# Moving tile addresses in a two-layer decoder trunk: large tiles on multiples of 2048 bytes, fourteen operand tiles in steps of 4128

## The chip, the cores and the metric

The kernel runs on one core of one Trainium2 chip. The metric is device microseconds of one execution; a run's figure is the median of several executions, and one separate execution is profiled.

## The reference

A decoder trunk on x of 512 tokens by 1024 channels, float32, two layers. Each layer is a half-step SwiGLU FFN, a token mixer, and a second half-step FFN:

```python
for layer in range(2):
    x = x + 0.5 * swiglu(rmsnorm(x, ffn_norm[layer, 0]), ffn_w_in[layer, 0], ffn_w_out[layer, 0])
    h = rmsnorm(x, mix_norm[layer])
    y = hybrid_mixer(h, ...) if layer == 0 else stick_breaking(h, ...)
    x = x + y
    x = x + 0.5 * swiglu(rmsnorm(x, ffn_norm[layer, 1]), ffn_w_in[layer, 1], ffn_w_out[layer, 1])
```

`swiglu(h)` is `(silu(a) * b) @ w_out` with `a, b` the halves of `h @ w_in`, 2816 wide. The hybrid mixer runs an RG-LRU recurrence beside forgetting attention with 8 heads; the other mixer is stick-breaking attention with 16 heads. Both attentions are causal.

## The kernel before

Everything is kept transposed: channels on the 128 partitions, the 512 tokens along the free dimension. x lies in eight tiles `x0` to `x7`. Every float32 operand is split into a high and a low part (`hi`/`lo` of weights, `h`/`l` or `xh`/`xl` of activations), and one product is three matmuls: high by high, high by low, low by high. The stationary operand of each is a 128x128 block of a weight tile, newly loaded for each matmul, and the moving operand is an activation tile; in the token products (`g_tok`, L241 to L243) it is the other way round.

The program is a row of stages: ffn(0), hybrid, ffn(1), ffn(2), stick, ffn(3). Inside each, TensorE's order is written out by hand (`manual_schedule`); the other engines follow by data.

- **ffn.** The hidden dimension is 22 blocks `j` of 128. Blocks 0 to 3 (`plain`) are ordinary products by `mm3` (L125 to L127) with moving operands of 512 columns. Blocks 4 to 21 come in nine pairs, each by seven products (`product`, L450) after Strassen's scheme: the operands `ops[0]` to `ops[6]` are computed once per ffn (`put`, `less`, `quarter`) and kept in fourteen tiles `t0h`, `t0l` to `t6h`, `t6l` of 128 x (4 x 256) floats; the weight sums are formed on VectorE per pair. One `product` is 24 matmuls of 256 columns. Between products come output units (`outputs`) for an earlier chunk: twelve matmuls of 512 columns by `mm3` per unit (eighteen in the last chunk), with hidden tiles `g` (and `sum` for blocks 20 and 21) as the moving operand.
- **hybrid and stick.** Projections as fill (`g_proj` L222 to L224 with 512 moving columns, `g_tok` L241 to L243 with 256 or 264), between the steps of `attend` (scores, transposes L639, `weigh` L657).
- `rstd_parts` (L163) multiplies sums of squares by a column of ones: a matmul of one column, with a full 128x128 weight load before each.

**Where tiles lie.** A tile's byte address within each partition follows from the order of the pools and, in a pool, from the order in which tags are first used; each slot is rounded up to 32 bytes. The first pool, `const`, begins at 1152 and ends at 3360. Then come `state` (x, `xh`, `xl`, `sq`, `acc`, two small `rt`, `rb`), `wp` (`raw`, `hi`, `lo`, 4096 bytes a slot), and the pool of the stage. So, modulo 2048:

| tiles | address mod 2048 | mod 512 |
|---|---|---|
| x, xh, xl, sq, acc; g of blocks 4 to 15 (they take the slots of xh, xl) | 1312 | 288 |
| weights raw, hi, lo; in the ffn: ab, a21, a22, sum, p5, the t tiles, g of blocks 0 to 3 and 16 to 19 | 1376 | 352 |
| hybrid and stick: many residues, as small and odd-sized tiles lie between large ones (tt of stick 1696, of hybrid 1792; v 1440) | | |

Blocks of a weight tile and quarters of a t tile start a multiple of 512 bytes into their tile, so the residue modulo 512 is the same for all blocks of one tile.

Of the kernel before, what the change touches and what calls it, by code (L numbers as in the profile page):

```python
# [10 lines left out]
F32 = mybir.dt.float32  # L11
F32R = mybir.dt.float32r
# [4 lines left out]
P = 128  # L17
S = 512
# [4 lines left out]
NB = S // P  # L23
HD = 64
# [12 lines left out]
QK0 = 80  # L37
FB0 = 82
NPAR = 90
NQF = 256 + H_FOX  # L40


# [25 lines left out]
def kernel(ctx: ExitStack, tc: tile.TileContext, x, par, ffn_in, ffn_in2, ffn_out, ffn_out2,  # L68
                      hy_ug, hy_qkv, hy_qf, rg_w, hy_out, sb_qk, sb_v, sb_out, out):
    nc = tc.nc  # L70
    V, A, G, T, SY = nc.vector, nc.scalar, nc.gpsimd, nc.tensor, nc.sync

    const = ctx.enter_context(tc.tile_pool(name="const", bufs=1))
    state = ctx.enter_context(tc.tile_pool(name="state", bufs=1))
    wp = ctx.enter_context(tc.tile_pool(name="wp", bufs=1))
    ps = ctx.enter_context(tc.tile_pool(name="ps", bufs=1, space=PSUM))
# [81 lines left out]
    def rstd_parts():  # L158

        pt = psum("t", 2)  # L160
        for tb in range(NB):
            for i, sq in enumerate(acc):
                T.matmul(out=pt[:, tb:tb + 1], lhsT=sq[:, tb * P:(tb + 1) * P], rhs=ones, start=i == 0, stop=i == 1)  # L163
        rt = state.tile([P, NB], F32, tag="rt", bufs=2, name="rt")
        V.tensor_scalar(out=rt, in0=pt[:, :NB], scalar1=1.0 / D, scalar2=EPS, op0=ALU.mult, op1=ALU.add)
        G.tensor_tensor(out=rt, in0=rt, in1=mhalf[:, :NB], op=ALU.pow)

        def rest():
            pb = psum("t", 2)
            for tb in range(NB):  # L170
                T.transpose(out=pb[:, tb * P:(tb + 1) * P], in_=rt[:, tb:tb + 1].broadcast_to([P, P]),
                            identity=ident)
            rb = state.tile([P, S], F32, tag="rb", bufs=1, name="rb")
            A.copy(out=rb, in_=pb)
            return rt, rb

        return rest
# [147 lines left out]
    def ffn(f, g_next, last=False):  # L325
# [2 lines left out]

        with ExitStack() as es:
            gp = es.enter_context(tc.tile_pool(name=f"ffn{f}", bufs=1))  # L330
            hid = {}
            ops = {}

            def slot(o, c, dt):

                return gp.tile([P, 4, 256], dt, tag=f"t{o}{c}", bufs=1, name=f"t{o}{c}")

            def temp(tag, dt=F32):
                return gp.tile([P, 2, S], dt, tag=tag, bufs={"sum": 4, "ab": 2}[tag], name=tag)
# [352 lines left out]
    def hybrid(g_next):  # L692
        with ExitStack() as es:
            mp = es.enter_context(tc.tile_pool(name="hy", bufs=1))

            def wk(tag, dt=F32, bufs=1):
                return mp.tile([P, S], dt, tag=tag, bufs=bufs, name=tag)

            rt = rb = None
# [4 lines left out]
            def r_in(i):  # L704
                def evac_u(pt):
                    nonlocal rt, rb
                    if rt is None:
                        rt, rb = rstd()
                    u = mp.tile([P, S + 4], F32, tag="u", bufs=2, name="u")
                    G.memset(u[:, 0:3], 0.0)  # L710
                    V.tensor_tensor(out=u[:, 3:3 + S], in0=pt, in1=rb, op=ALU.mult)
                    st[i] = [u]

                def evac_g(pt):
                    gs = wk("gs", bufs=2)
                    V.tensor_tensor(out=gs, in0=pt, in1=rb, op=ALU.mult)
                    st[i].append(gs)

                return [(1, 24 * US_512, g_proj(hy_ug[i + 4 * j], e, on_x, KT)) for j, e in enumerate((evac_u, evac_g))]

            def r_chain(i):

                u, gs = st[i]
                wraw = mp.tile([P, 2, P], F32, tag="wgr", name="wgr")
                wh = mp.tile([P, 2, P], F32R, tag="wgh", name="wgh")
                wl = mp.tile([P, 2, P], F32R, tag="wgl", name="wgl")
                G.memset(wraw, 0.0)
                for hb in range(2):
                    sl = slice(hb * HD, (hb + 1) * HD)
# [20 lines left out]
                o = wk("o")  # L750
# [6 lines left out]
                t = wk("c1")  # L757
                b = wk("c2")
# [53 lines left out]
            def forget():  # L812
                n = H_FOX
                ft, sp, sm, ww, pp = (f_in[0][:, 32 * q:32 * q + 32] for q in range(5))
                A.activation(out=sp, in_=ft, func=AF.Abs)
                A.activation(out=sm, in_=sp, func=AF.Sigmoid, scale=-1.0)
                A.activation(out=sp, in_=sp, func=AF.Sigmoid)
                log1p_exp(sp, sm, ww, pp)
                V.tensor_scalar(out=ft, in0=ft, scalar1=-1.0, scalar2=0.0, op0=ALU.mult, op1=ALU.max)
                yield  # L820
                V.tensor_tensor(out=ft, in0=ft, in1=sm, op=ALU.add)
                row = mp.tile([P, 6], F32, name="row")
                for r in range(4):
                    V.tensor_reduce(out=row[:, r:r + 1], in_=ident[:, r::32], axis=AX.X, op=ALU.add)
                for c in range(2):
                    V.tensor_tensor(out=row[:, 4 + c:5 + c], in0=row[:, 2 * c:2 * c + 1],
                                    in1=row[:, 2 * c + 1:2 * c + 2], op=ALU.add)
                V.tensor_scalar(out=row[:, 5:6], in0=row[:, 5:6], scalar1=-1.0, scalar2=None, op0=ALU.mult)
                for t in range(2):
                    nl = wk("ge" if t else "xc").rearrange("p (b g r) -> p b g r", b=NB, g=4)  # L830
                    V.tensor_copy(out=nl, in_=ft.rearrange("p (b h) -> p b h", h=n)[:, :, 4 * t:4 * t + 4]
                                  .unsqueeze(3).broadcast_to([P, NB, 4, 32]))
                    for _ in range(1 if t else HY_FORGET):
                        yield
                    pn = psum("t", 2)
                    for tb in range(NB):
                        T.transpose(out=pn[:, tb * P:(tb + 1) * P], in_=nl[:, tb].rearrange("p g r -> p (g r)"),
                                    identity=ident)
                    yield
                    nf, hi, mix = wk("c1"), wk("c2", F32R), wk("o")  # L840
                    V.tensor_tensor_scan(out=nf, data0=ones.broadcast_to([P, S]), data1=pn, initial=0.0,
                                         op0=ALU.mult, op1=ALU.add)
                    A.copy(out=hi, in_=nf)
                    V.tensor_tensor(out=nf, in0=nf, in1=hi.bitcast(F32), op=ALU.subtract)
                    for dst, r, c in ((fb[t], 0, 5), (fa[t], 2, 4)):
                        A.activation(out=mix, in_=hi.bitcast(F32), func=AF.Identity, scale=row[:, r:r + 1],
                                     bias=row[:, c:c + 1])
                        V.scalar_tensor_tensor(out=dst, in0=nf, scalar=row[:, r + 1:r + 2], in1=mix,
                                               op0=ALU.mult, op1=ALU.add)
                        yield  # L850
# [19 lines left out]
            def qk_unit(half, which, dst):  # L870
                qs = []

                def evac(tb, pt):
                    nonlocal rt, rb
                    if rt is None:
                        rt, rb = rstd()
# [1 line left out]
                        forget_in(tb, pt[:, 256:])  # L878
                        pt = pt[:, :256]
                    q = mp.tile([P, 256], F32, tag="q", bufs=8, name="q")  # L880
                    sq = mp.tile([P, 256], F32, tag="e0", bufs=1, name="sqq")
                    ss = mp.tile([P, 4], F32, tag="ss", bufs=4, name="ss")
                    rc = rt[:, tb:tb + 1]
                    A.activation(out=sq, in_=pt, func=AF.Square, scale=rc)
                    V.tensor_reduce(out=ss, in_=heads(sq), axis=AX.X, op=ALU.add)
# [41 lines left out]
            ls = {}  # L927

            def score(p, hb, b):
                n = (b + 1) * P  # L930
                if (hb, b) == (0, 0):
                    ls[p] = mp.tile([P, 2, NB], F32, tag="ls", bufs=2, name="ls")
                sp = pso()
                bs = slice(b * P, n)
                q2, k2 = (second[w][p % 2][hb] for w in range(2))
# [1 line left out]
                T.matmul(out=sp[:, bs], lhsT=identr, rhs=mask_c, start=False, stop=False, skip_group_check=True)  # L937
                T.matmul(out=sp[:, :n], lhsT=q2[:, bs], rhs=k2[:, :n], start=False, stop=True)
                sc = mp.tile([P, S], F32, tag="sc", bufs=3, name="sc")[:, :n]
                m = mp.tile([P, 1], F32, tag="m", bufs=4, name="m")  # L940
                V.tensor_reduce(out=m, in_=sp[:, :n], axis=AX.X, op=ALU.max, negate=True)
                A.activation(out=sc, in_=sp[:, :n], func=AF.Exp, bias=m, accum_out=ls[p][:, hb, b:b + 1])
                return sc
# [1 line left out]
            def finish(p, t):  # L945
                l = ls.pop(p)
                V.reciprocal(out=l, in_=l)
                ex = [mp.tile([P, 2, 2, HD], F32, tag=f"e{b}", bufs=1, name="ex") for b in range(2)]
                for b in range(2):
                    for hb in range(2):  # L950
                        G.tensor_copy(out=ex[b][:, :, hb, :],
# [84 lines left out]
            with tc.manual_schedule(engines={mybir.EngineType.PE}):  # L1036
                f = Fill(pre + jobs)
# [20 lines left out]
    def stick(g_next):  # L1058
        with ExitStack() as es:
            mp = es.enter_context(tc.tile_pool(name="sb", bufs=1))  # L1060

            def wk(name, bufs):
                return mp.tile([P, S + 4], F32, tag=name, bufs=bufs, name=name)

            y = {}
            rt = rb = None
            rs = mp.tile([P, 2, NB], F32, name="rs")
            qk, vv = {}, {}

            klo = [[mp.tile([P, S], F32R, name=f"kl{i}{c}") for c in "eo"] for i in range(2)]  # L1070
# [3 lines left out]
            def qk_tile(p):  # L1074
                def evac(j):
                    def go(pt):
                        nonlocal rt, rb
                        if rb is None:
                            rt, rb = rstd()
# [10 lines left out]
                            qk[p, j] = st  # L1090
                        else:

                            kt = wk("kt", 1)[:, :S]
                            V.tensor_tensor(out=kt, in0=pt, in1=rb, op=ALU.mult)
                            for t, l, a, b in zip(st, klo[p % 2], halves, halves[::-1]):
                                A.copy(out=t[a], in_=kt[a])
# [18 lines left out]
            def score(p, hb, b):  # L1115
# [3 lines left out]
                q, k = qk[p, 0][hb], qk[p, 1]  # L1119
# [1 line left out]
                T.matmul(out=sp[:, :n], lhsT=q[:, bs], rhs=klo[p % 2][hb][:, :n], start=False, stop=True)  # L1121
                be = wk("be", 4)[:, :n]
                nb = wk("nb", 2)[:, :n]
                c = wk("c", 2)
                A.activation(out=nb, in_=sp[:, :n], func=AF.Sigmoid, scale=rs[:, 1, b:b + 1])
                below(nb[:, bs], 1.0)
                A.activation(out=be, in_=sp[:, :n], func=AF.Sigmoid, scale=rs[:, 0, b:b + 1])
# [33 lines left out]
            f = Fill(jobs)  # L1161
# [82 lines left out]
```

## Time and profile before

| | |
|---|---|
| median of 3 runs | 1884.31 us (1884.13 to 1886.61) |
| the profiled execution | 1887.77 us, of which the span from first to last instruction 1886.1 |
| TensorE busy (matmul / weight load) | 1860.7 (99%) / 1675.6 (89%) us |
| VectorE / ScalarE / GpSimd busy | 1414.3 (75%) / 954.4 (51%) / 122.6 (7%) us |
| mean granted TensorE clock | 0.997 |
| DMA moved | 183.65 MB, queues busy 30% |

TensorE is called PE in the rows (PEld its weight loads), VectorE DVE, ScalarE ACT, GpSimd POOL, SyncE SP. Matmuls overlap, so the duration in a matmul's row (283 ns, 393 ns) is not what it costs; what it costs is the distance from its start to the start of the next, called its pace below.

### The profile page before, as it was taken

What the parts mean: (1) busy time and instruction counts of PE and PEld (TensorE: products, weight loads), DVE (VectorE), ACT (ScalarE), POOL (GpSimd) and SP (SyncE); (2) the same over time, 40 slices, a digit from 0 to 9 for tenths busy, and PEclk for the clock granted to TensorE, in tenths of its full rate; (3) what the DMA queues carried; (4) which work ended last, traced back from release to release, by engine and by line L of the source; (5) the groups of instructions that cost most, each with busy time, mean ns of one, the idle gap of its engine ahead of it and who ended that gap; (6) DMA issues with size and microseconds to landing.
All of it is one profiled execution on the core that took longest, in us unless ns stands there. A gap on an engine that the chain in (4) does not pass through costs nothing.

```text
span 1886.1 us, 29382 instructions
## 1 busy us (share of the span) xinstructions
PE 1860.7 (99%) x11818; PEld 1675.6 (89%) x11818; DVE 1414.3 (75%) x1892; ACT 954.4 (51%) x1399; POOL 122.6 (7%) x265
## 2 busy tenths in 40 slices
PE   8999999999999999999999999999999999999999
PEld 6899999898888899999889999988888888999997
DVE  8877676687878877677596777765889978767773
ACT  5444444466855444444444444444777654444441
POOL 2000000111100000000000000001333400000000
PEclk9999999998999999999999999999999999999999
DMA  5333332353333323332423333233212122333222
GB/s 181 99 101 99 101 110 70 96 163 96 83 99 100 101 92 100 101 108 75 132 69 112 112 101 97 83 101 101 68 56 68 57 94 96 100 107 101 96 74 95
DMA packets 57304, 183.65 MB, mean 97 GB/s; under 512 B 8016, under 2 KB 9296, under 8 KB 57168
## 3 DMA queue, kind: packets, MB, share of 16 engines
q1 hardware_dynamic: 57168, 181.77, 30.4%
q8 instruction: 93, 1.52, 0.3%
q14 instruction: 43, 0.35, 0.1%
HBM read 172.31 MB, written 2.10 MB: 92 GB/s over the span
## 4 chain that ended last, share of the span: by engine, by line
PE 90%; DVE 5%; issue 2%; ACT 1%; POOL 0%; DMA 0%; SPq 0%; DVEq 0%; POOLq 0%; ACTq 0%
PE mm L450 22%; PE s L450 11%; PE mm L125 6%; PE mm L126 6%; PE mm L127 6%; PE t L450 5%; PE po L127 4%; PE po L125 4%; PE po L126 4%; PE mm L241 2%; PE mm L242 2%; PE mm L243 2%; PE mm L222 2%; PE mm L223 2%; PE mm L224 2%
## 5 line engine op out<-in xcount | busy, mean ns | idle before, releaser
L440 DVE TENSOR_TENSOR lo_w<-sum,hi_w 128x1024 fp32r<-128x1024 f32 x144 | 176.0, 1224 | 100.1 <-ACT hi_w L439 99.2
L439 ACT CAST hi_w<-sum 128x1024 fp32r<-128x1024 f32 x144 | 150.6, 1048 | 198.3 <-PE mm L126 55.9
L117 ACT CAST hi_wo<-raw_wo 128x1024 fp32r<-128x1024 f32 (+1 forms) x96 | 93.9, 978 | 157.6 <-PE mm L126 66.0
L439 ACT CAST hi_w<-raw 128x1024 fp32r<-128x1024 f32 x72 | 75.7, 1052 | 136.4 <-PE s L450 71.4
L118 DVE TENSOR_TENSOR lo_wo<-raw_wo,hi_wo 128x1024 fp32r<-128x1024 f32 (+1 forms) x96 | 108.8, 1134 | 24.4 <-ACT hi_wo L117 24.4
L125 PE MATMUL mm<-g,hi_wo 128*128 128x512 f32 (+1 forms) x324 | 126.5, 391 | 0.0
L126 PE MATMUL mm<-g,hi_wo 128*128 128x512 f32 (+1 forms) x324 | 126.4, 390 | 0.0
L117 ACT CAST hi_w<-raw_w 128x1024 fp32r<-128x1024 f32 (+2 forms) x75 | 77.8, 1039 | 95.7 <-PE mm L126 43.9
L127 PE MATMUL mm<-g,lo_wo 128*128 128x512 f32 (+1 forms) x324 | 126.1, 389 | 0.0
L127 PE MATMUL po<-g,lo_wo 128*128 128x512 f32 x320 | 125.7, 393 | 0.4 <-DVE lo_wo L118 0.4
L125 PE MATMUL po<-g,hi_wo 128*128 128x512 f32 x320 | 126.0, 394 | 0.0
L126 PE MATMUL po<-g,hi_wo 128*128 128x512 f32 x320 | 125.8, 393 | 0.0
L118 DVE TENSOR_TENSOR lo_w<-raw_w,hi_w 128x1024 fp32r<-128x1024 f32 (+2 forms) x75 | 90.6, 1208 | 29.3 <-ACT hi_w L117 29.1
L542 DVE SCALAR_TENSOR_TENSOR x<-mm,x 128x512 f32<-128x512 f32 (+1 forms) x81 | 55.3, 683 | 54.6 <-PE mm L127 54.6
L241 PE MATMUL mm<-hi_w,xh 128*128 128x256 f32 (+1 forms) x312 | 90.6, 291 | 2.0 <-DVE q L889 2.0
L243 PE MATMUL mm<-hi_w,xl 128*128 128x256 f32 (+1 forms) x312 | 88.1, 282 | 0.0
L242 PE MATMUL mm<-lo_w,xh 128*128 128x256 f32 (+1 forms) x312 | 88.0, 282 | 0.0
L440 DVE TENSOR_TENSOR lo_w<-raw,hi_w 128x1024 fp32r<-128x1024 f32 x72 | 87.8, 1219 | 0.0
L456 DVE TENSOR_TENSOR sum<-a,a 128x1024 f32<-128x1024 f32 x36 | 44.1, 1225 | 55.5 <-DMA a<-in_dram 55.5
L542 DVE SCALAR_TENSOR_TENSOR x<-po,x 128x512 f32<-128x512 f32 x80 | 55.1, 689 | 40.4 <-PE po L127 40.4
L450 PE MATMUL t<-t1h,hi_w 128*128 128x256 f32 x288 | 81.5, 283 | 0.0
L450 PE MATMUL t<-t1l,hi_w 128*128 128x256 f32 x288 | 81.5, 283 | 0.0
(479 smaller groups left out, 6360.2 us busy)
## 6 DMA issues: line engine op xcount, KB each, us to landing
raw_w<-in_dram SPq DMA_DIRECT2D x72, 512.0 KB, 3.4
a<-in_dram SPq DMA_DIRECT2D x72, 512.0 KB, 3.5
raw<-in_dram SPq DMA_DIRECT2D x72, 512.0 KB, 3.5
raw_wo<-in_dram SPq DMA_DIRECT2D x64, 512.0 KB, 3.5
raw_wo<-in_dram SPq DMA_DIRECT2D x32, 384.0 KB, 3.1
raw_who<-in_dram SPq DMA_DIRECT2D x16, 512.0 KB, 3.3
qks<-hs SPq DMA_DIRECT2D x24, 128.0 KB, 2.5
x<-in_dram SPq DMA_DIRECT2D x8, 256.0 KB, 4.5
```

Of the source, the lines that this page charges most:

```text
L117: A.copy(out=hi[:, :n], in_=raw[:, :n])
L118: V.tensor_tensor(out=lo[:, :n], in0=raw[:, :n], in1=hi[:, :n].bitcast(F32), op=ALU.subtract)
L125: T.matmul(out=pt, lhsT=ah, rhs=bh, start=(start and i == 0), stop=False)
L126: T.matmul(out=pt, lhsT=ah, rhs=bl, start=False, stop=False)
L127: T.matmul(out=pt, lhsT=al, rhs=bh, start=False, stop=(stop and i == n - 1))
L241: T.matmul(out=pt, lhsT=ah, rhs=bh, start=(k == 0), stop=False)
L242: T.matmul(out=pt, lhsT=ah, rhs=bl, start=False, stop=False)
L243: T.matmul(out=pt, lhsT=al, rhs=bh, start=False, stop=(k == KT - 1))
L439: A.copy(out=hi, in_=src)
L440: V.tensor_tensor(out=lo, in0=src, in1=hi.bitcast(F32), op=ALU.subtract)
L450: T.matmul(out=po, lhsT=a, rhs=b[:, k], start=start and c + k + q == 0, stop=k == 3 and q == 2, skip_group_check=not (start and c == 0))
L542: V.scalar_tensor_tensor(out=xT[d][:, t], in0=po[:, t], scalar=0.5, in1=xT[d][:, t], op0=ALU.mult, op1=ALU.add)
```

## The change

Three new pools. `small`, opened right after `const`, takes tiles of a few bytes (`rt`, `row`, `ss`, `ls`, `m`, `rs`: fourteen slots of 32 bytes). `pad` holds 288 bytes that nothing reads. With these, 1152 + 2208 + 448 + 288 = 4096, so `state`, then `wp`, then each stage's main pool begin on a multiple of 2048; tiles of odd size in hybrid and stick go to a pool of their own behind it. In the ffn the fourteen t tiles move to a pool of their own behind the others, with 8 floats more each, so that one begins 4128 bytes after the one before, in the order t0h, t0l, t1h, t1l, t3h, t3l, t4h, t4l, t6l, t5h, t5l, t2h, t2l, t6h. Modulo 512 the first is at 0, the next at 32, then 64, up to 416. No instruction is added or taken away but one memset of the padding; shapes, order and engines stay.

```diff
+PAD = 72
...
+    small = ctx.enter_context(tc.tile_pool(name="small", bufs=1))
+    pad = ctx.enter_context(tc.tile_pool(name="pad", bufs=1))
+
+    G.memset(pad.tile([P, PAD], F32, name="pad"), 0.0)
...
-        rt = state.tile([P, NB], F32, tag="rt", bufs=2, name="rt")
+        rt = small.tile([P, NB], F32, tag="rt", bufs=2, name="rt")
...
+            gt = es.enter_context(tc.tile_pool(name=f"ffn{f}t", bufs=1))
...
-                return gp.tile([P, 4, 256], dt, tag=f"t{o}{c}", bufs=1, name=f"t{o}{c}")
+                t = gt.tile([P, 4 * 256 + 8], dt, tag=f"t{o}{c}", bufs=1, name=f"t{o}{c}")
+                return t[:, :4 * 256].rearrange("p (k s) -> p k s", s=256)
...
+            odd = es.enter_context(tc.tile_pool(name="hy_odd", bufs=1))
...
-                    u = mp.tile([P, S + 4], F32, tag="u", bufs=2, name="u")
+                    u = odd.tile([P, S + 4], F32, tag="u", bufs=2, name="u")
...
+            odd = es.enter_context(tc.tile_pool(name="sb_odd", bufs=1))
 
             def wk(name, bufs):
-                return mp.tile([P, S + 4], F32, tag=name, bufs=bufs, name=name)
+                return mp.tile([P, S], F32, tag=name, bufs=bufs, name=name)
...
-                c = wk("c", 2)
+                c = odd.tile([P, S + 4], F32, tag="c", bufs=2, name="c")
```

In the same way hybrid's `wgr`, `wgh`, `wgl`, `sqq` and `ex` go to `odd`, its `row`, `ss`, `ls`, `m` and stick's `rs` to `small`.

## Rows read from the trace of the kernel before

**Rows 1.** The page: busy time and share of each engine.

```profile
PE 1860.7 (99%) x11818; PEld 1675.6 (89%) x11818; DVE 1414.3 (75%) x1892; ACT 954.4 (51%) x1399; POOL 122.6 (7%) x265
```

**Rows 2.** Waits of TensorE over the span: total us, times, longest (largest four).

```profile
PE mm L125 <- ACT hi L316: 5.1, 1, 5.1
PE po L657 <- DVE tt L643: 4.0, 4, 1.3
PE mm L241 <- DVE q L889: 2.0, 1, 2.0
PE mm L127 <- DVE lo L317: 1.8, 2, 0.9
```

**Rows 3.** Busy time by stretch: PE, PEld, DVE, ACT, POOL, granted clock, DMA, GB/s.

```profile
420.00:440.00 20.00, 17.67 (x67) 13.81 (x66) 13.81 (x22) 14.01 (x23) 0.41 (x2) 0.83 0.50 136
...
925.00:1235.00 310.00, 310.00 (x2039) 283.37 (x2038) 230.38 (x260) 140.25 (x173) 1.01 (x1) 1.00 0.31 99
...
1300.00:1515.00 215.00, 209.35 (x1291) 184.13 (x1290) 187.09 (x318) 153.06 (x304) 73.73 (x190) 1.00 0.20 67
```

**Rows 4.** Groups by line and shape, one of each kind.

```profile
L125 PE MATMUL po<-g,hi_wo 128*128 128x512 f32 x320 | 126.0, 394 | 0.0
...
L241 PE MATMUL mm<-hi_w,xh 128*128 128x256 f32 x288 | 83.8, 291 | 2.0 <-DVE q L889 2.0
L450 PE MATMUL t<-t1h,hi_w 128*128 128x256 f32 x288 | 81.5, 283 | 0.0
...
L222 PE MATMUL mm<-xh,hi_w 128*128 128x512 f32 x192 | 81.0, 423 | 0.0
...
L125 PE MATMUL mm<-xh,hi_w 128*128 128x512 f32 x120 | 47.7, 398 | 0.0
```

**Rows 5.** Timeline, TensorE, one product: start, duration.

```profile
91.65 0.28 PE L450 MATMUL mm<-t0h,lo_w 128*128 128x256 f32 x1
...
100.05 0.40 PE L125 MATMUL mm<-g,hi_wo 128*128 128x512 f32 x1
```

**Rows 6.** Timeline, TensorE, last output chunk (g of 16 to 19, sum).

```profile
1856.60 0.39 PE L125 MATMUL mm<-sum,hi_wo 128*128 128x512 f32 x1
...
1877.00 0.39 PE L125 MATMUL po<-sum,hi_wo 128*128 128x512 f32 x1
```

**Rows 7.** Timeline, TensorE, an output chunk of blocks 4 to 15.

```profile
197.58 0.39 PE L125 MATMUL po<-g,hi_wo 128*128 128x512 f32 x1
...
201.08 0.39 PE L125 MATMUL mm<-g,hi_wo 128*128 128x512 f32 x1
```

**Rows 8.** Timeline, TensorE, projections with 512 columns of xh, xl.

```profile
417.12 0.39 PE L224 MATMUL mm<-xh,lo_w 128*128 128x512 f32 x1
...
421.08 0.40 PE L223 MATMUL mm<-xl,hi_w 128*128 128x512 f32 x1
```

**Rows 9.** Timeline, TensorE, token products, 256 columns of a weight tile.

```profile
1299.79 0.28 PE L241 MATMUL mm<-hi_w,xh 128*128 128x256 f32 x1
...
1303.91 0.28 PE L243 MATMUL mm<-hi_w,xl 128*128 128x256 f32 x1
```

**Rows 10.** Timeline, TensorE, token products after a row of transposes.

```profile
1375.57 0.28 PE L243 MATMUL mm<-hi_w,xl 128*128 128x256 f32 x1
...
1377.27 0.28 PE L243 MATMUL mm<-hi_w,xl 128*128 128x256 f32 x1
```

**Rows 11.** Timeline, TensorE, weight loads with one-column matmuls.

```profile
1538.03 1.70 PE L163 MATMUL t<-ones,sq 128*128 128x1 f32 x14
1539.59 0.48 PE L125 MATMUL mm<-xh,hi_w 128*128 128x512 f32 x1
```

**Rows 12.** Timeline, TensorE, token products at the lower clock.

```profile
454.71 0.41 PE L241 MATMUL mm<-hi_w,xh 128*128 128x256 f32 x1
454.92 0.41 PE L242 MATMUL mm<-lo_w,xh 128*128 128x256 f32 x1
455.14 0.41 PE L243 MATMUL mm<-hi_w,xl 128*128 128x256 f32 x1
455.35 0.41 PE L936 MATMUL s<-qks 128*128 128x256 f32 x1
```

**Rows 13.** Waits of ScalarE, 60 to 420 us.

```profile
ACT hi_w L439 <- PE s L450: 31.2, 15, 4.1
ACT hi_w L439 <- PE mm L450: 27.9, 17, 4.1
```

**Rows 14.** Groups on VectorE, an operand 4 bytes off, and none.

```profile
L481 DVE TENSOR_TENSOR ab<-s,keep 128x512 f32<-128x512 f32 x36 | 24.7, 685 | 2.9 <-PE s L450 2.9
...
L1132 DVE TENSOR_TENSOR be<-be,c 128x512 f32<-128x512 f32 x16 | 11.0, 684 | 0.0
```

**Rows 15.** The chip's core: span, mean granted clock.

```profile
core 0: 1886.1 us, clock 0.997
```

More of the change, by code (lines that the diff above doesn't have):

```diff
@@ L723, in r_chain @@
                 u, gs = st[i]
-                wraw = mp.tile([P, 2, P], F32, tag="wgr", name="wgr")
-                wh = mp.tile([P, 2, P], F32R, tag="wgh", name="wgh")
-                wl = mp.tile([P, 2, P], F32R, tag="wgl", name="wgl")
+                wraw = odd.tile([P, 2, P], F32, tag="wgr", name="wgr")
+                wh = odd.tile([P, 2, P], F32R, tag="wgh", name="wgh")
+                wl = odd.tile([P, 2, P], F32R, tag="wgl", name="wgl")
                 G.memset(wraw, 0.0)
@@ L821, in forget @@
                 V.tensor_tensor(out=ft, in0=ft, in1=sm, op=ALU.add)
-                row = mp.tile([P, 6], F32, name="row")
+                row = small.tile([P, 6], F32, name="row")
                 for r in range(4):
@@ L880, in evac @@
                     q = mp.tile([P, 256], F32, tag="q", bufs=8, name="q")
-                    sq = mp.tile([P, 256], F32, tag="e0", bufs=1, name="sqq")
-                    ss = mp.tile([P, 4], F32, tag="ss", bufs=4, name="ss")
+                    sq = odd.tile([P, 256], F32, tag="e0", bufs=1, name="sqq")
+                    ss = small.tile([P, 4], F32, tag="ss", bufs=4, name="ss")
                     rc = rt[:, tb:tb + 1]
@@ L931, in score @@
                 if (hb, b) == (0, 0):
-                    ls[p] = mp.tile([P, 2, NB], F32, tag="ls", bufs=2, name="ls")
+                    ls[p] = small.tile([P, 2, NB], F32, tag="ls", bufs=2, name="ls")
                 sp = pso()
@@ L939, in score @@
                 sc = mp.tile([P, S], F32, tag="sc", bufs=3, name="sc")[:, :n]
-                m = mp.tile([P, 1], F32, tag="m", bufs=4, name="m")
+                m = small.tile([P, 1], F32, tag="m", bufs=4, name="m")
                 V.tensor_reduce(out=m, in_=sp[:, :n], axis=AX.X, op=ALU.max, negate=True)
@@ L947, in finish @@
                 V.reciprocal(out=l, in_=l)
-                ex = [mp.tile([P, 2, 2, HD], F32, tag=f"e{b}", bufs=1, name="ex") for b in range(2)]
+                ex = [odd.tile([P, 2, 2, HD], F32, tag=f"e{b}", bufs=1, name="ex") for b in range(2)]
                 for b in range(2):
@@ L1060, in stick @@
             mp = es.enter_context(tc.tile_pool(name="sb", bufs=1))
+            odd = es.enter_context(tc.tile_pool(name="sb_odd", bufs=1))
             def wk(name, bufs):
-                return mp.tile([P, S + 4], F32, tag=name, bufs=bufs, name=name)
+                return mp.tile([P, S], F32, tag=name, bufs=bufs, name=name)
             y = {}
             rt = rb = None
-            rs = mp.tile([P, 2, NB], F32, name="rs")
+            rs = small.tile([P, 2, NB], F32, name="rs")
             qk, vv = {}, {}
@@ L1091, in go @@
                         else:
-                            kt = wk("kt", 1)[:, :S]
+                            kt = wk("kt", 1)
                             V.tensor_tensor(out=kt, in0=pt, in1=rb, op=ALU.mult)
```

## The prediction

> **What bounds the kernel now.** The page comes first: TensorE is busy 99% of the span, no other engine above 75% [rows 1]. The waits of TensorE are few and short; the largest is 5.1 us at the very start [rows 2]. In a stretch of pure FFN TensorE is busy throughout and VectorE 230 of 310 us; in stick VectorE is at 187 of 215 us, nearly the bound itself [rows 3]. ScalarE's casts of weights wait for TensorE to free a `hi` slot, not the other way [rows 13], so operands are ready ahead. So the time is the sum of the paces of 11,818 matmuls, and a change that alters only addresses acts through the pace or not at all. The paces, from start to start in the timeline:
>
> - seven products, 256 columns: 70 steps in 8.40 us, 120.0 ns [rows 5];
> - 512 columns, moving tile at 352 and weights at 352 (mod 512): 90 steps in 20.40 us, 226.7 ns [rows 6];
> - 512 columns, moving tile at 288, weights at 352: 15 steps in 3.50 us, 233.3 ns [rows 7]; the projections with xh, xl at 288 have 17 steps in 3.96 us, 232.9 ns [rows 8];
> - token products, 256 columns, moving at 352, weights at 288: 35 steps in 4.12 us, 117.7 ns [rows 9], and once, after transposes, 15 steps in 1.70 us, 113.3 ns at the same addresses [rows 10];
> - weight loads with one column of work: 14 in 1.56 us, 111 ns [rows 11].
>
> The reader is to see that rows 6 and rows 7 are the same instruction, shape and clock, on the same line, and differ by 6.7 ns. What differs between them is where the moving tile lies. I call **offset** the start of the weight block minus the start of the moving block, modulo 512: 0 in rows 5 and 6, 64 in rows 7 and 8, 448 in rows 9. At offset 0 the long matmul is at its fast pace, the short one at its slow pace. And 120 ns is above what either half needs: 111 ns for the weight load alone [rows 11], and about 107 ns for 256 columns alone, since at the lower level (1.2 GHz) the pace is 213 ns, 0.64 us for three steps [rows 12], and the full clock is twice that. So some 9 ns per short matmul are lost between the two streams, and 20 of the 233 ns of a long one (2 x 107 = 213).
>
> The Trainium skill (TensorE: Matmul & The Clock Gate, Part 2, step 1) says that the moving operand and the weight load have independent SBUF read ports, so that loading the next weights takes no bandwidth from the running matmul. By it addresses would not matter and the sum would be 0; the trace disagrees with 226.7 against 233.3 ns, so I go by the trace. That rule remains as a rival.
>
> **The change part by part.** After it, state, weights and the stage pools are at 0 modulo 512, and t0h at 0, the other thirteen t tiles at 32 to 416.
>
> 1. *512 columns in the FFN, offset 64 to 0.* Counts from the code and the groups [rows 4]: output units of three chunks, 8 x 4 x 3 x 3 = 288 per ffn, and the plain blocks, 4 x 2 x 8 x 3 = 192; times four ffns 1,920. Nearest row: rows 6, exactly that offset. 1,920 x 6.7 = 12.8 us; some at the start are paced by DMA, I take 12. Bounds: nothing, if the residue 352 itself and not the offset made rows 6 fast; and down to 213 ns, 20 x 1,920 = 39 us, if aligned starts also remove the rest, for which no row speaks.
> 2. *Projections L222 to L224, offset 64 to 0.* 576 matmuls [rows 4] x 6.3 = 3.6 us, but they are fill among attention steps, and two thirds are in stick, where VectorE sets much of the pace [rows 3]. I take half, 1.9 us; bounds 0 and 3.6.
> 3. *Token products, offset 448 to 0.* 960 matmuls, of the pace of rows 9, come to the offset of rows 5: 960 x 2.3 = 2.2 us lost. Bounds: 0, and as a gain 960 x 4.4 = 4.2 us if they fall into the pace of rows 10.
> 4. *Products, offset 0 to a multiple of 32.* 21 groups like that of rows 4 x 288 = 6,048 matmuls, by far the largest term: one ns is 6.0 us. No row has these fourteen offsets. The nearest rows with 256 columns and an offset other than 0 are rows 9 (117.7) and rows 10 (113.3). I take 117.7, as that is the pace which the same addresses nearly always settle in, and rows 10 a run that began after transposes: 6,048 x 2.3 = 13.9 us gained. Bounds: the weight load, 111.4 ns, 52 us gained; and, as the long matmul loses 6.7 ns by leaving offset 0 (rows 6 to rows 7), 126.7 ns, 40 us lost. VectorE's 230 of 310 us [rows 3] leave room for products 2% or 7% faster: it would go from 74 to at most 80%.
> 5. *At nothing.* VectorE and ScalarE instructions with new addresses: 684 ns with an operand 4 bytes off, 685 without [rows 14]. DMA landings: covered by casts that wait for TensorE anyway [rows 13]. The memset of the padding: GpSimd is idle 93% of the span [rows 1] and TensorE's first wait is for the first x tile and its split [rows 2]; uncovered it would be about 1 us. Stage pools that overlap others in a new way can move waits at five stage boundaries; all of TensorE's waits together are some 20 us, so 2 us either way. A few hundred matmuls (L257 to L259, L657) move both ways, under 1 us. A stretch at the lower clock level (0.83 in 420 to 440 us [rows 3]; 0.3% of the span off full clock [rows 15], all of it at half, is 10 us and costs 5) may shift, vanish or be joined by another: 5 us either way, a spread and no term.
>
> Sum: -12 - 1.9 + 2.2 - 13.9 = -25.6 us. Against the profiled execution's 1887.8 that is 1862; it is 3.5 above the median of the three runs, so the median becomes 1884.3 - 25.6 = 1859.
>
> **The rivals.**
>
> - *Products at the fast pace.* With the offset broken they settle at 113.3 (rows 10): 6,048 x 6.7 = 40.5, with terms 1 to 3 52 us: 1832. For it: rows 10 last 15 steps without a drift. Against: the same addresses give 117.7 elsewhere.
> - *Products unchanged, or half of it.* They stay at 120 because the loss lies in the alternation of two streams and not in the offset, and only terms 1 to 3 count: 1884.3 - 11.7 = 1873; about the same comes out if the products take 117.7 but the long matmuls stay at 233. For it: 120.0 without variation looks like a locked pattern. Against: no row with another offset shows it.
> - *Addresses do not matter.* Rows 6 and 7 then differ by something else, such as what the tiles held or what ran beside: 1884. This is what the skill's rule would give. Against: within rows 6 as within rows 7 the pace is constant while the other engines come and go.
> - *Slower: products at a worse offset.* The high and low tiles now differ by 32, so the offset changes with every matmul; if that costs the short ones what 64 costs the long ones, 120.0 becomes 126.7: +40.5 - 11.7 = +29, 1913. It turns into a loss of over 0.2% (3.8 us) from a pace of (11.7 + 3.8) / 6,048 = 2.6 ns above 120, 122.6. For it: rows 7, the one place where leaving 0 is shown, went up. Against: rows 9.
> - *Both better than any row at length.* Products at 111.4 and long matmuls near 220 (half way to 213): -52 - 7 x 2,496 more, with -12, about -80: 1804.
>
> **How the numbers follow.** Forecast 1859 (1854 to 1864 with clock and boundaries) 0.42; fast products 0.20; products unchanged or half 0.17; no effect 0.07; slower 0.09; better than the rows 0.05. 0.2% is 3.8 us, about what can be told from no change. Faster is the sum of the first three and the last, 0.84; same 0.07; slower 0.09. The range from 1827 to 1879 takes in the forecast, the fast products and the products unchanged with 5 us of spread, 0.79 together, and leaves out the ends.
>
> **What would show it.** In the profile after: the output units of blocks 4 to 15 at 226.7 from start to start, like those of rows 6; the projections alike; the token products at 120; the product's 24 steps at 2.82 us where they were 2.88 (2.72 if the fast rival is right, over 2.94 if the slow one is). The VectorE groups keep their means. The prediction is wrong if the products' pace differs by tile (the offsets run over fourteen values, and I have given them all one pace), if long matmuls at offset 0 do not take 226.7, or if the freed TensorE time turns into waits for VectorE.

## The result, and the profile after

The changed kernel takes 1865.72 us, median of 4 runs (1864.44 to 1868.59); the kernel before, beside it on the same chip, 1884.80 (1884.13 to 1886.61). The ratio is 0.9901, 95% interval 0.9889 to 0.9913: 19.1 us less. The forecast was 1859, the range 1827 to 1879.

The page of the changed kernel, and TensorE's two longest waits (total us, times, longest), which answer to [rows 1, 2]:

```profile
PE 1836.0 (99%) x11818; PEld 1664.1 (89%) x11818; DVE 1413.3 (76%) x1892; ACT 955.3 (51%) x1399; POOL 122.2 (7%) x266
```

```profile
PE mm L130 <- ACT hi L321: 5.3, 1, 5.3
PE po L664 <- DVE tt L650: 4.1, 4, 1.3
```

TensorE is still the bound, with the same number of matmuls; the waits are where they were and as long; GpSimd has one instruction more, the memset. So the gain lies in the paces. The same stretches as in [rows 3], windows of the changed kernel (PE, PEld, DVE, ACT, POOL, granted clock, DMA, GB/s):

```profile
420.00:440.00 20.00, 17.33 (x101) 14.84 (x100) 17.82 (x28) 15.44 (x27) 0.41 (x2) 1.00 0.45 126
925.00:1235.00 310.00, 310.00 (x2099) 286.81 (x2098) 231.43 (x262) 141.87 (x175) 1.14 (x3) 1.00 0.30 97
```

In the FFN stretch 2,099 matmuls fit where 2,039 did, and VectorE has 231 of 310 us, far from the bound. The first row shows the clock at 1.00 where the profile before had 0.83: that profiled execution carried a stretch at the lower level which this one has not.

Timeline of TensorE in the changed kernel, in that FFN stretch (start, duration): first matmul of each product, and of the output units between them.

```profile
997.23 0.28 PE L457 MATMUL mm<-t0h,hi_w 128*128 128x256 f32 x1
...
1000.04 0.28 PE L457 MATMUL mm<-t3h,hi_w 128*128 128x256 f32 x1
...
1002.87 0.28 PE L457 MATMUL t<-t1h,hi_w 128*128 128x256 f32 x1
...
1005.70 0.39 PE L130 MATMUL mm<-g,hi_wo 128*128 128x512 f32 x1
...
1008.46 0.28 PE L457 MATMUL s<-t4h,hi_w 128*128 128x256 f32 x1
...
1011.32 0.28 PE L457 MATMUL mm<-t5h,hi_w 128*128 128x256 f32 x1
```

A product is 24 steps. t0 takes 2.81 us (117.1 ns a step), t3 and t1 2.83 (117.9), t4 2.86 (119.2), against 120.0 in [rows 5]. The output unit, twelve steps, takes 2.76 us, 230.0 ns a step.

Timeline of an output chunk of blocks 4 to 15, the one of [rows 7]; then the last chunk, as in [rows 6]:

```profile
195.50 0.39 PE L130 MATMUL po<-g,hi_wo 128*128 128x512 f32 x1
...
197.57 0.39 PE L130 MATMUL po<-g,hi_wo 128*128 128x512 f32 x1
...
200.29 0.39 PE L130 MATMUL mm<-g,hi_wo 128*128 128x512 f32 x1
```

```profile
1842.09 0.39 PE L130 MATMUL mm<-sum,hi_wo 128*128 128x512 f32 x1
...
1855.69 0.28 PE L130 MATMUL mm<-g,hi_wo 128*128 128x256 f32 x1
```

The first nine steps take 2.07 us (230.0 ns), the next twelve 2.72 (226.7). So the long matmuls reach the forecast pace, but only some steps after a product. The last chunk, 60 steps in 13.60 us, is at 226.7, as before the change.

Timeline of projections with 512 columns, and of token products, which answer to [rows 8, 9]:

```profile
416.08 0.39 PE L227 MATMUL mm<-xh,hi_w 128*128 128x512 f32 x1
...
419.93 0.39 PE L229 MATMUL mm<-xh,lo_w 128*128 128x512 f32 x1
```

```profile
1281.94 0.28 PE L247 MATMUL mm<-lo_w,xh 128*128 128x256 f32 x1
...
1285.90 0.28 PE L247 MATMUL mm<-lo_w,xh 128*128 128x256 f32 x1
```

17 steps in 3.85 us are 226.5 ns (232.9 before); 33 steps in 3.96 us are 120.0 (117.7 before). VectorE's groups keep their means, as against [rows 14]:

```profile
L488 DVE TENSOR_TENSOR ab<-s,keep 128x512 f32<-128x512 f32 x36 | 24.7, 685 | 2.8 <-PE s L457 2.8
...
L1141 DVE TENSOR_TENSOR be<-be,c 128x512 f32<-128x512 f32 x16 | 10.8, 678 | 0.0
```

Adding up the distances from each matmul's start to the next one's, over the whole of either trace:

| matmuls | before, us | after, us | difference |
|---|---|---|---|
| products, 6,048 | 724.5 (119.8 ns each) | 714.9 (118.2) | -9.6 |
| `mm3` with 512 columns, 3,006 (2,862 in the FFN, 144 in hybrid and stick) | 711.9 | 701.8 | -10.1 |
| projections L227 to L229, 576 | 141.4 | 138.4 | -3.0 |
| token products, 960 | 117.7 | 117.9 | +0.2 |
| all others | 182.0 | 181.5 | -0.5 |

Together -22.8 before rounding; the spans differ by 22.7 (1886.1 to 1863.4). The medians differ by 19.1, since the profiled execution of before lies 3.0 above its median (1887.8, with the stretch at the lower clock) and that of after 0.6 below.

### The profile page after: what moved, and what is told of

Same layout as the page of the kernel before. It is cut to its first block, busy times and chain, and to the rows that moved or that the text cites. A ratio compares the mean times of both kernels' runs of the same rounds, so it can differ in the third digit from the quotient of the medians.

```text
span 1863.4 us, 29383 instructions
## 1 busy us (share of the span) xinstructions
PE 1836.0 (99%) x11818; PEld 1664.1 (89%) x11818; DVE 1413.3 (76%) x1892; ACT 955.3 (51%) x1399; POOL 122.2 (7%) x266
## 4 chain that ended last, share of the span: by engine, by line
PE 88%; DVE 6%; ACT 2%; issue 2%; POOL 1%; DMA 0%; SPq 0%; POOLq 0%; DVEq 0%; ACTq 0%
PE mm L457 22%; PE s L457 11%; PE mm L130 6%; PE mm L132 6%; PE mm L131 6%; PE t L457 5%; PE po L130 4%; PE po L132 4%; PE po L131 4%; PE mm L246 2%; PE mm L248 2%; PE mm L247 2%; PE mm L227 1%; PE mm L228 1%; PE mm L229 1%
## 5 line engine op out<-in xcount | busy, mean ns | idle before, releaser
L457 PE MATMUL s<-t4l,hi_w 128*128 128x256 f32 x288 | 81.6, 283 | 0.0
L457 PE MATMUL s<-t2l,hi_w 128*128 128x256 f32 x288 | 81.4, 283 | 0.0
```

Source lines behind the costliest of these rows:

```text
L457: T.matmul(out=po, lhsT=a, rhs=b[:, k], start=start and c + k + q == 0, stop=k == 3 and q == 2, skip_group_check=not (start and c == 0))
```

## The experiments

Below, a **start** is where a moving block begins, counted in bytes past a multiple of 256 from the weight blocks; it is the prediction's offset with the sign turned, and modulo 256. All weight blocks of a stream have one residue, so whether the block in use or the one loaded meanwhile matters, no run here tells. In the changed kernel it is 0 for the 512-column matmuls of the FFN, the projections and the token products of 256 columns; the t tiles have starts of their own. Four theories. *Offset*, mine: only this distance counts, and one distance has one pace. *Residue*: the absolute address modulo 512 counts. *Alternation*: what helps the products is that high and low tile differ, whatever they start at. *No effect*: addresses do nothing. Averages "over the trace" are of distances from start to start, as in the table above.

**Each half alone.** `align_only` has the alignment and lets the t tiles follow each other in steps of 4096, all at 0:

```diff
-                t = gt.tile([P, 4 * 256 + 8], dt, tag=f"t{o}{c}", bufs=1, name=f"t{o}{c}")
+                t = gt.tile([P, 4 * 256], dt, tag=f"t{o}{c}", bufs=1, name=f"t{o}{c}")
```

`step_only` is the kernel before with the t tiles alone changed:

```diff
+            gt = es.enter_context(tc.tile_pool(name=f"ffn{f}t", bufs=1))
...
-                return gp.tile([P, 4, 256], dt, tag=f"t{o}{c}", bufs=1, name=f"t{o}{c}")
+                t = gt.tile([P, 4 * 256 + 8], dt, tag=f"t{o}{c}", bufs=1, name=f"t{o}{c}")
+                return t[:, :4 * 256].rearrange("p (k s) -> p k s", s=256)
```

> The large tiles on multiples of 2048 bytes as in the changed kernel, but the fourteen t tiles in steps of 4096, all at 0 modulo 512 like the weights. Offset theory (the pace is set by the distance, modulo 512, between the moving block and the weight block that is loaded meanwhile): products back at 120.0 ns from start to start (118.2 in the changed kernel), long FFN matmuls still at 226.7; 6,048 x 1.8 = 11 us more than the changed kernel, 1876. Residue theory (aligned starts are what is fast): products at or below 118, 1866 or less. No effect of addresses: 1866, equal to the changed kernel.

> The kernel before with one edit: the fourteen t tiles in a pool of their own in steps of 4128 bytes, beginning at 352 modulo 512 like the weights. Offset theory: the products get the paces of the changed kernel (118.2 on average), the long matmuls keep 233.3; 9.6 us less than before, 1875. Residue theory: the products' starts are 352, 384, ... and not 0, 32, ..., so their paces are others than in the changed kernel, product by product. The two halves of the change add up: align_only and step_only together save what the whole change saves, about 19 us.

`align_only`: 1874.84 us (1874.11 to 1874.90), ratio 0.9948 (0.9931 to 0.9964), 10.1 us below before. Its timeline, products t0, t3, t1, then a unit:

```profile
1002.55 0.28 PE L457 MATMUL mm<-t0h,hi_w 128*128 128x256 f32 x1
...
1011.19 0.40 PE L130 MATMUL mm<-g,hi_wo 128*128 128x512 f32 x1
...
1013.93 0.28 PE L457 MATMUL s<-t4h,hi_w 128*128 128x256 f32 x1
```

72 steps in 8.64 us: 120.0 again, so the alignment does nothing to the products; twelve long ones in 2.74 (228.3). `step_only`: 1876.00 us (1875.11 to 1876.82), ratio 0.9955 (0.9940 to 0.9970), 9.0 below before; over the trace its products take 118.4 ns and the long matmuls of state tiles stay at 233.2. The halves add up: 10.1 + 9.0 = 19.1, the whole. One thing did not come as expected: t0, at the same two starts in both kernels, took 117.0 ns in all 36 products of the changed kernel (after the first six steps), but 119.8 in 25 of the 36 of `step_only`, where most long matmuls before it have another start. So already here the distance alone did not settle a pace.

**Distance or address.** `shift352` moves everything behind the padding by 352 bytes:

```diff
-PAD = 72
+PAD = 160
```

> The changed kernel with 352 bytes more of padding: every large tile moves together, so all offsets stay and all residues modulo 512 become 352. Offset theory: the same time as the changed kernel (within 2 us) and the same pace for each product. Residue theory: the long matmuls leave 226.7 or the products 118.2 by more than 1 ns on average, 4 us or more.

1866.02 us (1864.79 to 1866.56), ratio 0.9901 (0.9886 to 0.9916). Timeline, the same place as in the changed kernel:

```profile
996.80 0.28 PE L457 MATMUL mm<-t0h,hi_w 128*128 128x256 f32 x1
...
1005.27 0.39 PE L130 MATMUL mm<-g,hi_wo 128*128 128x512 f32 x1
...
1008.03 0.28 PE L457 MATMUL s<-t4h,hi_w 128*128 128x256 f32 x1
```

8.47 us for three products and 2.76 for the unit, to the hundredth what the changed kernel has; over the trace both kernels' products take 118.21 ns. Residue falls for this shift; the distance, which stayed, accounts for the paces.

**Which starts are good.** Three kernels place each ffn's t tiles and its hidden tiles of blocks 0 to 3 and 16 to 19 at starts of their own, from tables `RES` (high and low, per product) and `GRES`:

```diff
-                t = gt.tile([P, 4 * 256 + 8], dt, tag=f"t{o}{c}", bufs=1, name=f"t{o}{c}")
-                return t[:, :4 * 256].rearrange("p (k s) -> p k s", s=256)
+                t = gt.tile([P, 4 * 256 + 128], dt, tag=f"t{o}{c}", bufs=1, name=f"t{o}{c}")
+                r = RES[f][o][c == "l"] // 4
+                return t[:, r:r + 4 * 256].rearrange("p (k s) -> p k s", s=256)
...
-                    h, l = (gp.tile([P, S], F32R, tag=f"g{c}{j % 4}", name="g") for c in "hl")
+                    q = GRES[f] // 4
+                    h, l = (gt.tile([P, S + 128], F32R, tag=f"g{c}{j % 4}", name="g")[:, q:q + S] for c in "hl")
```

`scan_a` takes equal pairs, pairs 256 apart, and neighbours 32 apart; `scan_b` one pair per ffn: (192, 192), (192, 448), (160, 160), (160, 192); `scan_c` 192, 32 and 160 with others.

> The changed kernel with every t tile in a larger slot, so that its start can be set freely: in ffn 0 and 1 and two products of ffn 2 the high and the low tile of a product have the same start modulo 512 (0, 32, ... 480, one per product); in the rest of ffn 2 they differ by 256, in ffn 3 by 32. The hidden tiles of blocks 0 to 3 and 16 to 19 start at 128, 256, 384, 448 in ffn 0 to 3. Offset theory: with equal starts the products at a start other than 0 run at 116 to 119 ns, at 0 at 120.0; long matmuls with moved hidden tiles run slower than 226.7, up to 233. Alternation theory (the gain comes from the high and low tiles differing, not from their distance to the weights): all products with equal starts at 120.0, those that differ faster.

> Freely set starts again (modulo 512, high tile / low tile), now one pair for all seven products of an ffn: 192/192 in ffn 0, 192/448 in ffn 1, 160/160 in ffn 2, 160/192 in ffn 3; hidden tiles of blocks 0 to 3 and 16 to 19 at 32, 96, 160, 224. In the first scan two paces stood at the same starts 192/192: 113.3 when another product came just before, 117.7 when long matmuls did. If the pace is a state that the streams settle in and that is kept while starts do not change, ffn 0 and 1 show 113.3 or 117.7 for whole stretches, by what came before; if each product chooses anew, the first steps decide product by product. With a period of 256 the first two ffns are alike. Long matmuls at 32, 96, 160, 224: between 226.7 and 233 if 0 is the best start, below 226.7 somewhere if not.

> Freely set starts: ffn 0 has the high tiles at 192 and the low ones at 0, 32, 64, 96, 128, 160, 224; ffn 1 the low ones at 192 and the high ones at those seven; ffn 2 the high ones at 32 and ffn 3 at 160 with the low ones at the other seven. Hidden tiles of blocks 0 to 3 and 16 to 19 at 192, 64, 16, 240. Offset theory: both distances count, each pair has a pace of its own between 113 and 122; if only the high tiles' distance mattered (two of three matmuls move them), the paces in ffn 0 would all be those of 192.

1869.94, 1865.33 and 1871.71 us, one execution each. What they are for is the pace by start, over the traces, after the first six steps of a product (the mean, or the values between which single products split); long matmuls are those that ran without a wait:

| start of both, mod 256 | 0 | 32 | 64 | 96 | 128 | 160 | 192 | 224 |
|---|---|---|---|---|---|---|---|---|
| product, ns | 120.0 | 116.7 or 117.8 | 117.8 | 119.9 | 118.8 or 120.0 | 117.2 to 118.8 | 113.3 or 117.7 | 118.2 |
| long matmul, ns | 228 | 233.3 | 229.9 | 233.6 | 232.6 | 234.0 | 233.3 | 233.3 |

Starts 256 apart, 192 aside, give the same in the mean, most within 0.4 ns and 160 against 416 by 1.4, no more than `scan_b` shows within 160 alone (0 and 256 mixed 119.9; 64 with 320 117.8). So the period is 256 bytes, not the 512 that I had counted in; [rows 9] at distance 448 is a start of 64 (117.8 here, 117.7 there), and [rows 7] at distance 64 is a start of 192 (233.3 in both). Alternation falls: equal high and low starts run at 116.8 in the mean at 32 and at 117.8 at 64, as quick as unequal ones; only at 96 and in part at 128 are they near the 120.0 of 0. Mixed pairs lie between 117 and 121.

Some columns have two values, that of 192 the furthest apart, and `scan_b` shows them at the same addresses. Its timeline in the first ffn, first a unit whose hidden tiles start at 32, five products, a double unit at 0, two products, a double unit at 0:

```profile
116.08 0.39 PE L132 MATMUL mm<-g,hi_wo 128*128 128x512 f32 x1
...
118.88 0.28 PE L461 MATMUL mm<-t0h,hi_w 128*128 128x256 f32 x1
...
132.48 0.39 PE L132 MATMUL po<-g,hi_wo 128*128 128x512 f32 x1
...
137.93 0.28 PE L461 MATMUL s<-t2h,hi_w 128*128 128x256 f32 x1
...
143.59 0.39 PE L132 MATMUL po<-g,hi_wo 128*128 128x512 f32 x1
```

The unit at 32 runs at 233.3 ns (2.80 us for 12), the 120 steps behind it take 13.60 us, 113.3 ns. The unit at 0 runs at 227.1 (5.45 us for 24), and the 48 steps behind it take 5.66, 117.9. So products at 192 have two paces that last, and what ran before chooses: in the first two ffns 30 products take 113.3, all in stretches behind units at 32 or 96, and the other 96 take 117.8. With that, Offset falls as far as it says that one distance has one pace. I called this the *Entry* theory and went on with it.

**All t tiles at 192.** `t192` is the changed kernel with one start for all fourteen:

```diff
-                t = gt.tile([P, 4 * 256 + 8], dt, tag=f"t{o}{c}", bufs=1, name=f"t{o}{c}")
-                return t[:, :4 * 256].rearrange("p (k s) -> p k s", s=256)
+                t = gt.tile([P, 4 * 256 + 128], dt, tag=f"t{o}{c}", bufs=1, name=f"t{o}{c}")
+                return t[:, 48:48 + 4 * 256].rearrange("p (k s) -> p k s", s=256)
```

> The changed kernel with all fourteen t tiles at 192 modulo 512 instead of at fourteen different starts. In the scan the products at 192/192 took 117.7 ns after long matmuls whose moving tiles lay at 0 and 113.3 after long ones at 32. Entry theory (the pace is a state of the two streams that the long matmuls before hand on): here all long ones are at 0, so all products at 117.7; 6,048 x 0.45 = 3 us less than the changed kernel, 1863. If the state were chosen by chance or by the tiles themselves, part of the products would take 113.3: 1840 to 1860.

1860.19 us (1859.60 to 1860.81), ratio to before 0.9869 (0.9854 to 0.9884), 5.5 us better than the changed kernel. Timeline, three products and a unit:

```profile
994.62 0.28 PE L457 MATMUL mm<-t0h,hi_w 128*128 128x256 f32 x1
...
1003.10 0.39 PE L130 MATMUL mm<-g,hi_wo 128*128 128x512 f32 x1
...
1005.82 0.28 PE L457 MATMUL s<-t4h,hi_w 128*128 128x256 f32 x1
```

72 steps in 8.48 us (117.8) and twelve in 2.72 (226.7): the long matmuls are at their settled pace from the first step, where behind the fourteen starts of the changed kernel they took 230.0. Over the trace: products -2.8 us, long ones -3.0. The second gain was not in the expectation. Two of the 252 products take 113.3 all the same, though every long matmul is at 0: t5 in ffn 2 and 3, each behind a unit that took 2.87 us in place of 2.72.

**What must run before.** `mark32` and `mark64` are `t192` with every fourth hidden tile and every fourth xh, xl at 32 or 64, so that a unit ends on three such matmuls; `state64` has all activations at 64. The line that sets it (the tiles of `state` are moved by small unused tiles between them):

```diff
-                    h, l = (gp.tile([P, S], F32R, tag=f"g{c}{j % 4}", name="g") for c in "hl")
+                    q = 8 if j % 4 == 3 else 0
+                    h, l = (gt.tile([P, S + 128], F32R, tag=f"g{c}{j % 4}", name="g")[:, q:q + S] for c in "hl")
```

> t tiles at 192 as in the run beside it, and every fourth hidden tile (blocks 3, 7, 11, 15, 19, with xh3, xl3, xh7, xl7, whose slots they take) at 32 modulo 256, so that each output unit and each plain block ends on long matmuls that are not at 0; the others stay at 0. Entry theory: the products come in by the fast way, 113.3 instead of 118.2: 6,048 x 4.9 = 30 us less; about 700 marked long matmuls cost 6 ns more, 4 us: 1840. If only the distance of the product's own tiles counts, products stay at 117.7 and the time is 1867.

> As the run beside it, with the marked tiles at 64 modulo 256 instead of 32; long matmuls at 64 took 229.9 ns in the scan, those at 32 233.3. Entry theory with any start other than 0 as the fast way in: products at 113.3 and 2 us less for the marked matmuls, 1838. If 64 is no fast way in, products at 117.7: 1865.

> t tiles at 192, and all activation tiles (x, xh, xl, every hidden tile but sum) at 64 modulo 256, the weights at 0. Long matmuls at 229.9 instead of 228.4 on average, some 3,500 of them: 5 us more; token products at an offset other than 0: 2 us less. If 64 is a fast way in, products at 113.3: 30 us less, 1839 in all; if not, 117.7 and 1866.

1871.46 us (ratio 0.9933, 0.9916 to 0.9949), 1869.03 (0.9916, 0.9901 to 0.9931) and 1865.48 (0.9896, 0.9881 to 0.9910): all worse than `t192`, and the products at 117.7 in all three, but for three single products of `mark32` and one of `state64` at 113.3. `mark32` and `mark64` are 4 us above even the slower of their two forecasts: the long matmuls cost 10.4 and 8.2 us more than in `t192`, where I had put 4 and 2 for the marked ones alone. Timeline of `mark32`:

```profile
1001.20 0.28 PE L462 MATMUL mm<-t0h,hi_w 128*128 128x256 f32 x1
...
1009.68 0.39 PE L130 MATMUL mm<-g,hi_wo 128*128 128x512 f32 x1
...
1012.47 0.28 PE L462 MATMUL s<-t4h,hi_w 128*128 128x256 f32 x1
```

72 steps in 8.48 us, 117.8, though each unit ended on three matmuls at 32 and ran at 232.5 (2.79 us for 12). The theory in the form "the last block must not start at 0" falls, and so does "a unit slower than 227 is enough".

`state64` has a second place with a start of 192: in its token products the moving operand is the weight tile, at 0, and the stationary one a block of the activations, at 64. Here 96 steps run from matmuls of 264 columns, with no long one just before, to the first long one:

```profile
374.12 0.28 PE L247 MATMUL mm<-hi_w,xh 128*128 128x256 f32 x1
...
385.00 0.39 PE L228 MATMUL mm<-xh,hi_w 128*128 128x512 f32 x1
```

10.88 us, 113.3 ns. So the quick pace does not need long matmuls at 32 ahead of it. For the products, left was a longer run at 32. `state32` has all activations and the hidden tiles of blocks 0 to 3 at 32, by wider padding ahead of `state` and of the weights; `half32` the third and fourth of each four, so that a unit ends on six. `state32` against `t192`, then `half32` against `mark32`:

```diff
-PAD = 72
+PAD = 80
...
+    G.memset(wp.tile([P, 56], F32, name="pad2"), 0.0)
...
+                    q = 8 if j < 4 else 0
```

```diff
-                    q = 8 if j % 4 == 3 else 0
+                    q = 8 if j % 4 >= 2 else 0
```

> All fourteen tiles of the products stand at 192 past a multiple of 256 bytes, all activations that the output units and projections read (the hidden tiles of blocks 0 to 3 among them) at 32, the weights at 0; nothing of the arithmetic is changed. Entry theory in its present form (a whole run of matmuls at 32 ahead of the products hands on the quicker of the two paces, as in the run with the products' tiles at 192 where the hidden tiles stood at 32): products at 113.3 ns, 6,048 x 4.4 = 27 us less than with the tiles at 192 alone, long matmuls at 233 in place of 227, 2,880 x 5.8 = 17 us more: about 1850 us. If such a run does not hand it on: products 117.7, about 1877 us. No effect of addresses: 1860 us.

> Tiles of the products at 192; of each eight hidden tiles and of each eight tiles of the input halves the third, fourth, seventh and eighth stand at 32 past a multiple of 256 bytes, the others at 0; the arithmetic is unchanged. Entry theory, if some matmuls in a row at 32 ahead of the products are enough: products at 113.3 ns (-27 us against the tiles at 192 alone), half of the long matmuls 5.8 ns longer (+9 us): about 1842 us. If they are not enough: products 117.7 ns, about 1869 us.

`state32`: 1848.92 us (1848.48 to 1849.40), ratio 0.9807 (0.9791 to 0.9823). `half32`: 1848.68 (1847.59 to 1850.47), ratio 0.9808 (0.9793 to 0.9822). Timelines of `state32` (five products, double unit) and `half32` (three products, unit):

```profile
1017.98 0.28 PE L459 MATMUL mm<-t0h,hi_w 128*128 128x256 f32 x1
...
1031.58 0.39 PE L131 MATMUL po<-g,hi_wo 128*128 128x512 f32 x1
...
1037.18 0.28 PE L459 MATMUL s<-t2h,hi_w 128*128 128x256 f32 x1
```

```profile
991.69 0.28 PE L462 MATMUL mm<-t0h,hi_w 128*128 128x256 f32 x1
...
999.85 0.39 PE L130 MATMUL mm<-g,hi_wo 128*128 128x512 f32 x1
...
1002.63 0.28 PE L462 MATMUL s<-t4h,hi_w 128*128 128x256 f32 x1
```

13.60 us for 120 steps and 8.16 for 72: 113.3 in both. The long matmuls pay: 233.3 in `state32` (5.60 us for 24) and 231.7 in `half32` (2.78 for 12). Over the traces against `t192`, products -25.2 and -24.8 us, long ones +13.1 and +12.8. For `half32` I had put the long ones at +9; those that start at 0 do not stay at 227 but average 230 among neighbours at 32. Behind output units that end on six or more matmuls at 32 every product of the two kernels takes 113.3; behind units that end on three, three of 252 do. But a run at 32 is not enough by itself. In each ffn of `state32` the first three products stand behind plain blocks whose long matmuls are all at 32. In ffn 1, the last 24 of these and the 72 steps of the products:

```profile
613.03 0.40 PE L131 MATMUL s<-xh,hi_w 128*128 128x512 f32 x1
...
618.63 0.28 PE L459 MATMUL mm<-t0h,hi_w 128*128 128x256 f32 x1
...
627.11 0.39 PE L131 MATMUL po<-g,hi_wo 128*128 128x512 f32 x1
```

The long ones take 233.3 ns (5.60 us for 24), as the units do, and the products behind them 117.8 (8.48 for 72). That is so in all four ffns of `state32` (12 products) and in ffn 1 of `half32` (3), whose plain block ends on six at 32. What in the sequence chooses the pace is therefore not isolated by these runs. Both versions beat both kernels: 36 us (1.9%) below before, 17 us below the changed kernel.

## Why the prediction was right, point by point

- **The bound.** Right: waits unchanged, and the difference of the spans is that of the paces. By addresses alone the ratio went to 0.9901 with the change and to 0.9807 with `state32`. The Trainium skill (TensorE: Matmul & The Clock Gate, Part 2, step 1) gives moving operand and weight load separate read ports, so that the load takes no bandwidth from the matmul; read as in the prediction, that nothing changes with addresses, it disagrees with these runs. The steps of [rows 12], from which I took the pace at the lower clock, do stand at a granted clock of 0.50 (454 to 456 us).
- **Term 1, long matmuls.** Right in mechanism; -10.1 us measured against -12 (-8.4 against `step_only`, whose state tiles lie as before). The 226.7 holds where they run at length, but the first steps behind a product take about 230; `t192` gives 3.0 us of it back.
- **Term 2, projections.** -1.9 forecast, -3.0 measured, of which some is the stretch at the lower clock in the profile before: against `step_only`, whose profile has less of it (0.91 in 420 to 440 us), whose activations lie as before and whose projections take 141.0 us, it is -2.6. By the pace alone it could have been -3.6; I had taken half.
- **Term 3, token products.** +2.2 forecast; the pace went to 120.0 as said. In sum +0.2, and +1.5 against `step_only` (116.4 us), for the same reason.
- **Term 4, products.** The term that was mis-sized: -13.9 forecast, -9.6 measured. I gave fourteen offsets the one pace of [rows 9], 117.7. The seven products have 117.1 (t0) to 119.1 (t2) over the trace, 118.2 in the mean. And I started from 120.0, where the mean before, with the first steps behind long matmuls, was 119.8: 6,048 x 1.6 = 9.6. The prediction named paces that differ by tile as a sign that it is wrong; on this point it was.
- **The rival of fast products** (113.3, [rows 10]) did not occur in the changed kernel, but I put it aside for a reason that was only half right. A pace of 113.3 need be no transient behind transposes: in `state32` and `half32` it holds in 240 and 249 of 252 products, in `scan_b` in 30, and in `state64` for 96 token products in a row. All these have a start of 192. Rows 10 have 64, where all 18 equal products of `scan_a` took 117.8; what started rows 10 was not tried.
- **Slower, and no effect**: excluded for this change. Of all pairs of starts scanned the slowest took 121.0 ns (high at 128, low at 192), short of the 122.6 from which the change would have lost.
- **Sum.** -25.6 forecast, -19.1 measured by the medians, and -22.7 between the two profiled executions; the profile before, with its stretch at the lower clock, makes 3.0 of the difference. Against the -22.7 the terms missed both ways: products by 4.3 us and long matmuls by 1.9 too much forecast, projections by 1.1, token products by 2.0 and the rest by 0.5 too little. That they cancel in part was luck.

What stays open: why distances modulo 256 act at all, and what in the sequence chooses between 113.3 and 117.7. The length of a run at 32 sorts the products behind output units, but not those behind plain blocks, nor the token products of `state64`. A kernel with products at 113.3 and all long matmuls at 226.7, which by `t192` less 25 us would be about 1835 (an estimate), was not found: in `scan_b` a unit at 0 ends the quick pace.

## What to carry to other kernels

In a kernel whose time is the sum of matmul paces, read the pace from start to start by tile, and compare places where only the address differs; here 120, 117.7 and 113.3 ns stood in one trace ahead of any change. What counted here was the distance of moving block and weight block modulo 256 bytes, together with what ran before: long moving operands were best at 0, 256-column ones at 192 or 32. One good start for all operands of the products (192, 1860 us) did better than a spread (1866), and one bad one (0, 1875) worse. Measure in the real sequence: a start that is worse for one kind (233 in place of 227 ns) can come with a gain in another, as in `state32`.

## What the runs showed of the hardware that was not expected

- The same matmul at the same addresses and the full clock has two paces that last, 113.3 and 117.7 ns. Which of them it takes depends on what ran before, in a way that these runs did not isolate; either was kept through all 120 steps of a stretch of products. Long matmuls have such a pair too: in ffn 3 of `scan_c`, at 240, units run at 226.7 or at about 236.
- The period is 256 bytes, and steps of 16 or 32 bytes matter: a long matmul takes about 228 ns at 0, 231.7 at 16, 233.3 at 32 and 229.9 at 64.
- Moving all large tiles together by 352 bytes changes nothing (1866.02 against 1865.72 us).
